# Handing a part's recurrences to the scheduler after 9 of 25 projection units instead of 13, at 2.5 steps per unit instead of 2

## The chip, the cores and the metric

The kernel runs on one core of a Trainium2 chip. The metric is the device time of one execution in microseconds; the times below are those of several executions, and the profile is of one more.

## The reference, cut to what matters

One layer over 2,048 tokens with 16 learned tokens ahead of them (T = 2,064) and a width of 1,024. The normalised input goes through one projection whose 3,080 columns are shared by three mixers; their outputs go through one output projection, and then follows a gated feed-forward net of width 2,816 with a depthwise convolution over time.

```python
p = rms_norm(h, norm_mix_pre) @ w_in
pa = p[..., :A_COLS]                    # RG-LRU group, 512 columns
pb = p[..., A_COLS:A_COLS + B_COLS]     # forgetting attention: q, k, v (512 each) and 8 gates
pc = p[..., A_COLS + B_COLS:]           # RWKV-7 group, 1024 columns
oa = rg_lru_group(xa, ya, ...)          # h_t = a_t * h_(t-1) + b_t, width 256
ob = forgetting_attention_group(...)    # 8 heads of 64, softmax(q k + c_i - c_j), causal
oc, v_own = rwkv7_group(pc, ...)        # S = S * w - (S kk) (kk a) + v k, 4 heads of 64x64
mixed = jnp.concatenate([oa, ob, oc], axis=-1) @ w_out
h = h + rms_norm(mixed, norm_mix_post)
f = causal_dwconv(rms_norm(h, norm_ffn_pre) @ ffn_up, ffn_conv)
h = h + rms_norm((gelu(gate) * val) @ ffn_down, norm_ffn_post)
```

The two recurrences (LRU and RWKV-7) run over time, so a block of tokens needs the state that the block before it left. RWKV-7 is computed in chunks of 64 tokens, whose inner triangular systems are solved by substitution.

## The kernel before, in words

Every large product is made in three matmuls of split operands (`mm3`, lines 170 to 174: high x high, high x low, low x high), recorded on TensorE under lines L172 to L174.

**The projection** (tile `psp`) runs in three parts of the tokens, each in two blocks of 400 and 384, of 384 and 384, and of 256 and 256 columns. A part is the generator `w_in_part` with 25 units: first the gates of attention (unit 1), then 8 column tiles of the RWKV group (kind "c", units 2 to 9), 4 of the LRU group (kind "a", units 10 to 13), 4 tiles of k, 4 of v and 4 of q; the last two units take one block each of the last two q tiles. The weight tile of a unit is split into a high and a low half in part 0 (`load_parts`, lines 161 to 167, ScalarE and VectorE) and stored; parts 1 and 2 load the halves again. Results leave PSUM over ScalarE or VectorE and go to DRAM (`scr_p`, `scr_v`, `scr_qh` and others).

**The recurrences** (PSUM tiles `rps` and `eps`) are the generator `recurrences`: two gate blocks of attention, then for each of three blocks of 256 tokens the first half of an RWKV block up to `R.SOLVED` (the raw rows of the projection are loaded, mixed with the token before, decays are made, the small triangular systems solved on GpSimd and VectorE with two round trips of DMA, `da` and `dx`), then the second half of the block before it (`R.ending`: the inverses of 64x64 by many 32x32 matmuls of line L1176, the state, the output), and then the LRU of the same block. Each `yield` ends a step. The last block (8) has 64 tokens.

`Beside` deals these steps out: `advance` is called once for each unit and takes `PACE` steps, as long as there are any. A part's recurrences are added to it when the unit READY + 1 of the same part has been made; in part 0, the first READY units are made ahead of the constants and of this loop. Steps that are left over go on with the units of the next part, and after part 2 `beside.finish()` and the loop over `R.ending` emit the rest.

**What emission decides.** The program is built with a scheduler: the order in which the code emits instructions is their priority, and the scheduler places them on the engines' queues by when it takes their operands to be ready. On the chip each engine then runs its queue in that order.

**Attention** (tiles `mx`, `sc`, `po`) is emitted after the recurrences. It runs in two halves: for all 8 heads the query blocks 0 and 1, and then for all heads the blocks 2 and 3, whose keys are twice as long. It takes the memory that the projection's pools leave. The output projection's weights (`woh`, `wol`, 16 loads of 512 KB, line L1480) and its PSUM take the space of the recurrences' pools (`rec.close()`); its tiles (`pswo`) are computed in the second half of attention, as attention makes their rows, and the last of them after it. After that come the feed-forward up (`psu`) and down (`psd`) products.

Of the kernel before, what the change touches and what calls it, by code (L numbers as in the profile page):

```python
# [438 lines left out]
class Attn:  # L439
# [43 lines left out]
    def next(self, s):  # L483
        self.turn[s] = (self.turn[s] + 1) % len(self.ring[s])
        return self.ring[s][self.turn[s]]
# [898 lines left out]
def lru_block(core, R, scr, k, b):  # L1384

    nc = core.nc
    t0 = max(0, Rwkv.start(b))
    n = min(T, Rwkv.start(b + 1)) - t0
    c0 = PAD + t0
    tt = nc.vector.tensor_tensor  # L1390
    stt = nc.vector.scalar_tensor_tensor

    def tl(s):
        return R.t([P, 256], s)[:, :n]

    def raw(row, a):
        t = R.t([P, 260], "lraw", bufs=2)[:, : c0 + n - a]
        nc.sync.dma_start(t, scr["p"][row : row + P, a : c0 + n])
        return t

    for p in range(2):
        pc = slice(p, p + 1)
        x = raw(P * p, c0 - 3)
        u, r, g, al = (tl("l" + s) for s in ("u", "r", "g", "a"))
        nc.scalar.activation(u, x[:, 3:], AF.Identity, scale=k["conv_w"][:, 6 + p : 7 + p], bias=k["conv_b"][:, pc])
        for i in range(3):
            stt(u, x[:, i : n + i], k["conv_w"][:, 2 * i + p : 2 * i + p + 1], u, op0=ALU.mult, op1=ALU.add)


        ps = R.pe()  # L1410
        pa, px = ps[:, :n], ps[:, 256 : 256 + n]
        nc.tensor.matmul(pa, k["ga_w"][:, p], u, start=True, stop=True)
        nc.tensor.matmul(px, k["gx_w"][:, p], u, start=True, stop=True)
        nc.scalar.activation(r, pa, AF.Abs, bias=k["ga_b"][:, pc])
        nc.vector.tensor_scalar(al, pa, k["ga_b"][:, pc], 0.0, op0=ALU.add, op1=ALU.min)
        nc.scalar.activation(g, px, AF.Tanh, scale=0.5, bias=k["rate"][:, 2, pc])
        nc.scalar.activation(r, r, AF.Tanh, scale=0.5)
        nc.scalar.activation(al, al, AF.Exp)
        stt(r, r, 1.0, al, op0=ALU.add, op1=ALU.mult)
        stt(g, g, 1.0, u, op0=ALU.add, op1=ALU.mult)  # L1420
        yield
        nc.scalar.activation(al, r, AF.Exp, scale=k["rate"][:, 0, pc])
        nc.scalar.activation(r, r, AF.Tanh, scale=k["rate"][:, 1, pc])

        tt(u, al, al, op=ALU.mult)
        stt(r, u, 1.0, r, op0=ALU.add, op1=ALU.mult)
        nc.vector.tensor_scalar(r, r, 1e-34, None, op0=ALU.max)
        nc.scalar.activation(r, r, AF.Sqrt)
        stt(g, g, 0.5, r, op0=ALU.mult, op1=ALU.mult)
        nc.vector.tensor_tensor_scan(u, al, g, k["h"][:, pc], op0=ALU.mult, op1=ALU.add)  # L1430
        nc.vector.tensor_copy(k["h"][:, pc], u[:, n - 1 : n])

        ya, y = raw(2 * P + P * p, c0), r
        nc.scalar.activation(y, ya, AF.Square)
        nc.vector.tensor_scalar(y, y, 0.044715, 1.0, op0=ALU.mult, op1=ALU.add)
        tt(y, y, ya, op=ALU.mult)
        nc.scalar.activation(y, y, AF.Tanh, scale=0.7978845608028654)
        stt(y, y, 1.0, ya, op0=ALU.add, op1=ALU.mult)
        stt(u, u, 0.5, y, op0=ALU.mult, op1=ALU.mult)
        nc.sync.dma_start(scr["mix"][P * p : P * p + P, t0 : t0 + n], u)  # L1440
        yield
# [466 lines left out]

READY = 13
PACE = 2.0

WIDE = (0, 5)

# [32 lines left out]
            pass  # L1948


def recurrences(core, R, lk, f_bias, scr, blocks, part):


    for blk in blocks:
        gate_block(core, R, f_bias, scr, blk[2])
        yield
    for b in ((0, 1, 2), (3, 4, 5), (6, 7, 8))[part]:
        gen = R.block(b)
        while next(gen) != R.SOLVED:
            yield  # L1960
        yield from R.ending
        R.ending = gen
        yield from lru_block(core, R, scr, lk, b)


# [10 lines left out]
def hybrid_block_kernel(ctx: ExitStack, tc: tile.TileContext, args, out):  # L1976
    a = {s: v[0] if s != "meta_tokens" else v for s, v in args.items()}
    nc = tc.nc
    core = Core(tc, ctx)
    scr = scratch(tc, ctx, core)  # L1980
# [4 lines left out]
    def run(gen):  # L1985
        for _ in gen:
            pass

    def pool(es, name, bufs, **kw):
        return es.enter_context(tc.tile_pool(name=name, bufs=bufs, **kw))  # L1990
# [11 lines left out]
    with ExitStack() as p1:  # L2002
        core.const = pool(p1, "const1", 1)
        dp = pool(p1, "dp", 2, space=DRAM)
        rec = ExitStack()
        ps_rw = pool(rec, "ps_rw", 2, space=PSUM, **right)
        ps_ae = pool(rec, "ps_ae", 1, space=PSUM, **right)
        gp = pool(rec, "gp", 1, **right)
        rp = pool(rec, "rp", 1, **right)
        with ExitStack() as p1a:  # L2010
            ps_mm = pool(p1a, "ps_mm", 5, space=PSUM)
            g_pre = spread(pool(p1a, "gpre", 1), a["norm_mix_pre"], "g_pre")
            pools = {"xn": pool(p1a, "xn", 1), "nt": pool(p1a, "nt", 4), "w": pool(p1a, "w", 2), "st": pool(p1a, "st", 2)}
            sums = up_sums(core, pool(p1a, "us", 1), a["ffn_up"], scr, EARLY)
            split_out = w_out_split(core, pools["nt"], a["w_out"], scr)
            following = w_in_norm(core, pools, ps_mm, x, meta, g_pre, 0)
            for part in range(3):
                blocks = following
                if part == 0:
                    zeros = pools["st"].tile([P, PAD], F32, tag="sth", name="zeros")  # L2020
                    nc.vector.memset(zeros[:], 0.0)
                    for r in range(0, A_ROWS + C_ROWS, P):
                        nc.gpsimd.dma_start(scr["p"][r : r + P, 0:PAD], zeros[:])
                units = w_in_part(core, pools, ps_mm, a["w_in"], blocks, scr, part)
                for _ in range(READY if part == 0 else 0):
                    next(units)
                if part == 0:
                    attn_consts(core)
                    rk = rwkv_consts(
                        core, gp, ps_ae,  # L2030
                        {
                            s[5:]: (v.rearrange("h d -> (h d)") if s == "rwkv_r_k" else v)
                            for s, v in a.items() if s.startswith("rwkv_")
                        },
                    )
                    lk = lru_consts(
                        core, gp, ps_ae,
                        {
                            "conv_w": a["lru_conv_w"], "conv_b": a["lru_conv_b"], "ga_w": a["lru_gate_a_w"],
                            "ga_b": a["lru_gate_a_b"], "gx_w": a["lru_gate_x_w"], "gx_b": a["lru_gate_x_b"],  # L2040
                            "lam": a["lru_lambda"],
                        },
                    )
                    columns(core, gp, ps_ae, [a["ffn_conv"].rearrange("i (r p) -> (i r) p", p=P)], "", cw)
                    R = Rwkv(core, rp, dp, ps_rw, ps_ae, scr, rk)
                    beside = Beside(PACE)
                for i, _ in enumerate(units, READY + 1 if part == 0 else 1):
                    if i == READY + 1:
                        beside.add(recurrences(core, R, lk, a["fox_f_bias"], scr, blocks, part))
                    beside.advance()  # L2050
                    if part and (i % 2 == 0 or part == 1 and i > 1):
                        with tc.issue_after(core.loaded.ins):
                            next(split_out if i % 2 else sums, None)
                run(sums) if part == 2 else None
                if part < 2:
                    following = w_in_norm(core, pools, ps_mm, x, meta, g_pre, part + 1)
        beside.finish()
        for _ in R.ending:
            pass
        rec.close()  # L2060
        p2 = ExitStack()
        ps_wo = [pool(p2, "ps_wo", 2, space=PSUM, **right)]
        with ExitStack() as p1b:
            more = pool(p1b, "ps_more", 1, space=PSUM, **right, **early)
            at = Attn(core, pool(p1b, "ap", 2, **early), pool(p1b, "ps_at", 1, space=PSUM), more, scr)

            pool(p1b, "pad", 1, **right).tile([P, 24832], F32, name="pad")
            at.run(pool(p1b, "mt", 1, **right, **early))
# [145 lines left out]
```

## Time and profile before

| what | value |
|---|---|
| median of the runs | 3072.16 us |
| lowest of the runs | 3068.99 us |
| span of the profiled execution (first to last instruction) | 3071.8 us |
| TensorE busy | 2921.6 us, 95% |
| VectorE busy | 2054.8 us, 67% |
| ScalarE busy | 1482.3 us, 48% |
| GpSimd busy | 1358.8 us, 44% |
| mean granted TensorE clock | 0.969 |
| moved by DMA | 532.58 MB, 173 GB/s in the mean |

The profile lists the span of its execution and no other time of it; the span lies 0.4 us from the median of the runs.

How the rows are read. In the page, each digit of a row of slices is the busy share of one fortieth of the span in tenths. A row of a stretch has its start and end, its length, then for each engine busy microseconds with the count of instructions, then the granted clock of TensorE, the share of the DMA engines and GB/s. A row of a tile has the least, the median and the greatest duration in ns, the first and the last start in us, and shapes. A row of waits reads: engine, tile and line of what waited, what ended the wait, microseconds in total, how often, the longest. PE is TensorE's matmul, PEld its weight load, DVE VectorE, ACT ScalarE, POOL GpSimd, SP SyncE, whose queue issues nearly all transfers. A matmul of plain float32 leaves two records.

### The profile page before, as it was taken

The numbers are of one execution on the slowest core, as the hardware profiler recorded it, in microseconds if no ns is written. First come the engines' busy times: TensorE is split into PE (matmuls) and PEld (weight loads), VectorE is DVE, ScalarE is ACT, GpSimd is POOL, SyncE is SP. The second block draws the span as 40 slices with busy tenths as digits, with TensorE's granted clock in tenths as the row PEclk, the third lists the DMA queues.
The fourth block names the chain that finished last, engine by engine and source line by source line (L and its number), as shares of the span: only waits on it lengthen the run. The fifth ranks groups of instructions, "written<-read, shape, count | busy, mean of one in ns | idle before, by whom it ended". The sixth has DMA issues, their size and how long they took to land. (4 is left out here: it accounts for less than half of the span.)

```text
span 3071.8 us, 52793 instructions
## 1 busy us (share of the span) xinstructions
PE 2921.6 (95%) x18694; PEld 2495.2 (81%) x18694; DVE 2054.8 (67%) x3934; ACT 1482.3 (48%) x2853; POOL 1358.8 (44%) x1589
## 2 busy tenths in 40 slices
PE   6999999999989999999989899999999999999998
PEld 6998898888876654665558899999999998787876
DVE  5268645656667785556635788888778786547766
ACT  4245332443336553555534656666566665324333
POOL 1001121122114555667842457445655444547765
PEclk9998999999988898999999999999999999999999
DMA  6776578466654346535245555566777765435444
GB/s 211 244 237 207 161 244 287 156 211 204 196 153 94 88 104 199 133 99 122 62 129 173 168 182 180 169 201 208 214 215 216 219 189 171 161 104 171 149 160 144
DMA packets 467818, 532.58 MB, mean 173 GB/s; under 512 B 85488, under 2 KB 355514, under 8 KB 466000
## 3 DMA queue, kind: packets, MB, share of 16 engines
q1 hardware_dynamic: 467168, 528.81, 56.5%
q8 instruction: 147, 2.41, 0.3%
q14 instruction: 119, 0.97, 0.1%
q0 software_dynamic: 384, 0.39, 0.0%
HBM read 369.11 MB, written 159.95 MB: 172 GB/s over the span
## 5 line engine op out<-in xcount | busy, mean ns | idle before, releaser
L172 PE MATMUL psu<-xo,uw 128*128 128x344 f32 x1848 | 589.9, 323 | 16.7 <-ACT xo L1594 6.9
L173 PE MATMUL psu<-xo,uw 128*128 128x344 f32 x1848 | 592.6, 321 | 0.0
L174 PE MATMUL psu<-xo,uw 128*128 128x344 f32 x1848 | 582.9, 320 | 0.0
L172 PE MATMUL psp<-xh,wh 128*128 128x384 f32 (+2 forms) x1152 | 383.6, 333 | 4.1 <-ACT wh L166 2.4
L174 PE MATMUL psp<-xh,wl 128*128 128x384 f32 (+2 forms) x1152 | 380.7, 331 | 3.5 <-DMA wl<-scr_wk 3.5
L173 PE MATMUL psp<-xl,wh 128*128 128x384 f32 (+2 forms) x1152 | 380.5, 330 | 0.0
L172 PEld LDWEIGHTS psu<-xo,uw 128*128 128x128 f32 x1848 | 346.9, 188 | 20.3 <-ACT xo L1594 7.1
L1595 DVE TENSOR_TENSOR uw<-uq,uw 128x512 fp32r<-128x512 f32 x341 | 316.2, 933 | 70.3 <-ACT uw L1594 63.7
L173 PEld LDWEIGHTS psu<-xo,uw 128*128 128x128 f32 x1848 | 347.9, 188 | 0.3 <-DVE xo L1595 0.3
L174 PEld LDWEIGHTS psu<-xo,uw 128*128 128x128 f32 x1848 | 346.5, 188 | 0.0
L1594 ACT ACTIVATE uw<-uq 128x512 fp32r<-128x512 f32 x462 | 287.9, 627 | 110.1 <-PE psu L174 48.7
L686 ACT ACTIVATE p<-sc,bias 128x512 f32<-128x512 f32 (+4 forms) x352 | 195.8, 590 | 178.5 <-PE sc L682 146.3
L1725 DVE SCALAR_TENSOR_TENSOR uy<-psu,ffn_cols,uy 128x342 f32<-128x342 f32 (+1 forms) x396 | 223.9, 567 | 60.7 <-ACT uy L1723 59.1
L559 DVE TENSOR_REDUCE mc<-mx 128x1 f32<-128x512 f32 (+6 forms) x352 | 190.3, 565 | 100.9 <-PE mx L554 75.8
L1731 POOL TENSOR_TENSOR uy<-uy,uy 128x342 f32<-128x342 f32 (+1 forms) x132 | 140.6, 1065 | 253.2 <-DVE uy L1725 77.4
L725 POOL TENSOR_TENSOR acc<-acc,p 128x512 f32<-128x512 f32 (+3 forms) x208 | 221.8, 1068 | 60.3 <-ACT p L686 23.9
L1595 POOL TENSOR_TENSOR uw<-uq,uw 128x512 fp32r<-128x512 f32 x121 | 177.9, 1470 | 125.0 <-ACT uw L1594 92.7
L174 PEld LDWEIGHTS psp<-xh,wl 128*128 128x128 f32 x1152 | 222.1, 193 | 13.0 <-issue 6.1
L172 PEld LDWEIGHTS psp<-xh,wh 128*128 128x128 f32 x1152 | 222.1, 193 | 10.7 <-issue 4.0
L173 PEld LDWEIGHTS psp<-xl,wh 128*128 128x128 f32 x1152 | 222.1, 193 | 7.6 <-issue 5.5
L1595 DVE TENSOR_TENSOR fo<-u,fo 128x896 fp32r<-128x896 f32 x88 | 112.6, 1279 | 121.3 <-ACT fo L1594 121.3
L1594 ACT ACTIVATE fo<-u 128x896 fp32r<-128x896 f32 x88 | 81.1, 922 | 206.3 <-POOL u L1841 106.8
(465 smaller groups left out, 6470.4 us busy)
## 6 DMA issues: line engine op xcount, KB each, us to landing
uq<-scr_us SPq DMA_DIRECT2D x220, 256.0 KB
uq<-in_ffn_up_dram SPq DMA_DIRECT2D x209, 256.0 KB
wl<-scr_wk SPq DMA_DIRECT2D x48, 512.0 KB
wh<-scr_wk SPq DMA_DIRECT2D x48, 512.0 KB
u<-scr_ff SPq DMA_DIRECT2D x88, 256.0 KB
scr_ff<-uy SPq DMA_DIRECT2D x110, 171.0 KB
raw<-in_w_in_dram SPq DMA_DIRECT2D x24, 512.0 KB
scr_wk<-wh SPq DMA_DIRECT2D x24, 512.0 KB
```

Source lines behind the costliest of these rows:

```text
L172: nc.tensor.matmul(out, ah, bh, start=first, stop=False, skip_group_check=more)
L173: nc.tensor.matmul(out, ah, bl, start=False, stop=False, skip_group_check=more)
L174: nc.tensor.matmul(out, al, bh, start=False, stop=last, skip_group_check=more)
L559: self.reduced = nc.vector.tensor_reduce(mc[:rows, i, ci : ci + 1], ps[:rows, : e - a], axis=AX.X, op=ALU.max)
L686: last = nc.scalar.activation(p[:rows, :w], ps[:rows, :w], AF.Exp, bias=bias[:rows, j : j + 1])
L725: eng.tensor_tensor(a, ps_[0][0][:rows, c0:n] if start and i == 1 else a, p[:rows, : n - c0], op=ALU.add)
L1594: core.nc.scalar.activation(hi, src, AF.Copy)
L1595: (eng or core.nc.vector).tensor_tensor(lo, src, hi, op=ALU.subtract)
L1725: stt(y[:, :n], src[:, i : n + i], cw[:, 44 * i + cc : 44 * i + cc + 1], y[:, :n], op0=ALU.mult, op1=ALU.add)
L1731: core.pooled = nc.gpsimd.tensor_tensor(v[:, :n], g[:, :n], v[:, :n], op=ALU.mult)
```

## The change

READY goes from 13 to 9, so a part's recurrences are added when unit 10 has been made and not unit 14; in part 0 the constants, too, are emitted after 9 units and not after 13. PACE goes from 2 to 2.5 steps for a unit. As the LRU needs the column tiles of kind "a", which are made in units 10 to 13, `recurrences` gets a list `made` with the units made in each part, and yields without work ahead of each LRU block while fewer than WHOLE = 13 are made. The arithmetic is the same.

```diff
-READY = 13
-PACE = 2.0
+READY = 9
+WHOLE = 13
+PACE = 2.5
...
-def recurrences(core, R, lk, f_bias, scr, blocks, part):
+def recurrences(core, R, lk, f_bias, scr, blocks, part, made):
...
         yield from R.ending
         R.ending = gen
+        while made[part] < WHOLE:
+            yield
         yield from lru_block(core, R, scr, lk, b)
...
             following = w_in_norm(core, pools, ps_mm, x, meta, g_pre, 0)
+            made = [0, 0, 0]
             for part in range(3):
...
                 for i, _ in enumerate(units, READY + 1 if part == 0 else 1):
+                    made[part] = i
                     if i == READY + 1:
-                        beside.add(recurrences(core, R, lk, a["fox_f_bias"], scr, blocks, part))
+                        beside.add(recurrences(core, R, lk, a["fox_f_bias"], scr, blocks, part, made))
                     beside.advance()
```

## The prediction

> **What bounds the kernel now.** I read the page first: the span, the busy shares and the slices of TensorE with its granted clock.
>
> ```profile
> span 3071.8 us, 52793 instructions
> PE 2921.6 (95%) x18694; PEld 2495.2 (81%) x18694; DVE 2054.8 (67%) x3934; ACT 1482.3 (48%) x2853; POOL 1358.8 (44%) x1589
> ...
> PE   6999999999989999999989899999999999999998
> ...
> PEclk9998999999988898999999999999999999999999
> ```
>
> TensorE is busy for 95% of the span and no other engine is above 67%, so the time is TensorE's work plus what it loses: 150 us idle, and some lowered clock, both mostly left of the middle. The clock's dip, slices 12 to 16 of about 77 us, is where the recurrences end. So I asked for busy time by stretch: start of the recurrences, the projection beside them, the first 53 us after the projection, the rest of the recurrences beside attention, the load of the output weights, and attention with output tiles.
>
> ```profile
> core 0: us, PE busy (x) PEld busy (x) DVE busy (x) ACT busy (x) POOL busy (x), PEclk, DMA share, GB/s
> 200.00:250.00 50.00, 50.00 (x300) 45.70 (x300) 33.75 (x85) 30.28 (x58) 8.26 (x16) 1.00 0.60 184
> 250.00:300.00 50.00, 42.73 (x291) 39.05 (x291) 42.91 (x117) 25.99 (x50) 4.40 (x6) 0.83 0.70 242
> 300.00:897.00 597.00, 577.52 (x5381) 521.77 (x5380) 351.85 (x884) 231.76 (x456) 118.67 (x194) 0.97 0.62 200
> 897.00:950.00 53.00, 40.52 (x347) 28.35 (x345) 45.20 (x118) 22.45 (x50) 21.84 (x29) 0.84 0.71 151
> 950.00:1148.00 198.00, 184.76 (x1651) 122.71 (x1644) 156.21 (x420) 116.64 (x252) 109.18 (x181) 0.91 0.36 91
> 1148.00:1202.00 54.00, 46.43 (x189) 22.63 (x188) 31.29 (x71) 16.35 (x32) 19.89 (x26) 0.75 0.87 256
> 1202.00:1400.00 198.00, 195.94 (x882) 122.70 (x882) 111.38 (x231) 98.81 (x178) 135.59 (x186) 1.00 0.44 110
> ```
>
> The columns are stretch, length, busy us with count, then granted clock. I call "loss" the idle time plus (1 - clock) times the length. It is 7.3 + 8.5 = 15.8 us in 250-300; 19.5 + 17.9 = 37.4 in 300-897, so 53 us for the projection from 200 on; 12.5 + 8.5 = 21 in 897-950; 13.2 + 17.8 = 31 in 950-1148 (15.7%); 7.6 + 13.5 = 21 in 1148-1202; and 2.1 in 1202-1400 (1%). Recurrence work beside attention thus loses most, attention alone almost nothing. The stage limits are in the rows of the single tiles:
>
> ```profile
> L174 PE MATMUL psp<-xh,wl x1152: 274/337/736, 42.5 to 896.0; 128*128 128x384 f32 x96, 128*128 128x256 f32 x64, 128*128 128x400 f32 x32
> ...
> L1034 PE MATMUL eps<-rwwa,wa_up x72: 272/376/502, 174.5 to 978.2; 64*128 64x256 f32 x64, 64*128 64x64 f32 x8
> ...
> L1321 PE MATMUL rps<-rwsg,g_up x36: 275/379/564, 373.2 to 1147.5; 128*128 128x256 f32 x32, 128*128 128x64 f32 x4
> ...
> L681 PE MATMUL sc<-q,k x352: 170/392/796, 908.8 to 1564.7; 128*128 128x512 f32 x112, 128*128 128x272 f32 x16, 128*16 128x16 f32 x16, 128*128 128x400 f32 x16
> ...
> L1480 SPq DMA_DIRECT2D woh<-scr_wo x8: 320/430/1478, 1164.1 to 1187.6; - x8
> ```
>
> The projection (psp) ends at 896, the recurrences (eps, rps) run from 174.5 to 1147.5, attention (sc) begins at 908.8, and the output weights, whose buffers need the recurrences' space, load from 1164.1.
>
> **The change part by part.** No instruction's work is added or removed; steps are moved in emission. Counted in the code: part 0 of the recurrences has 40 steps, parts 1 and 2 have 47 each, and 7 close the last block. Before, each part advances 12 units of 2 steps after its start and uses its other units for the backlog; 16 steps stay over after part 0, 23 after part 1, and 30 come after the last unit. After, 16 units of 2.5 steps give 40: about 1 and 7 stay over, and 14 come after the last unit. The wait for WHOLE costs one empty step, in part 0; later the previous block's seven closing steps carry the recurrence past unit 13 anyway.
>
> What counts is where the scheduler puts them. In the two built orders of TensorE I counted the matmuls of the recurrences and gates (2,304 in all) and of attention (1,762). Ahead of the last projection matmul stand 1,646 before and 1,745 after; by thirds of the projection 62, 697 and 757 become 246, 632 and 714. Behind it stand 658 recurrence matmuls among 610 of attention before, 559 among 364 after. So 30 steps less 14 come down to 99 matmuls. The front of block 7, few matmuls and a long chain on VectorE and GpSimd, is what mainly crosses. The first output-tile matmul stands behind 771 attention matmuls before, 720 after.
>
> The prices, rows of one tile each: rps for the projection and for the recurrences beside attention, then the same for eps.
>
> ```profile
> 150.00:897.00 747.00, 165.25 (x2935) 139.32 (x2936) 74.78 (x154) 40.27 (x80) 0.97 0.64 207
> 897.00:1148.00 251.00, 71.80 (x1232) 58.49 (x1228) 31.90 (x79) 14.57 (x31) 0.90 0.44 104
> ```
>
> ```profile
> 150.00:897.00 747.00, 62.51 (x223) 33.06 (x223) 22.86 (x56) 27.45 (x66) 0.97 0.64 207
> 897.00:1148.00 251.00, 10.86 (x40) 6.70 (x40) 4.02 (x11) 4.11 (x12) 0.90 0.44 104
> ```
>
> Beside the projection 227.8 us of TensorE for 1,646 is 0.138 us each; beside attention 82.7 us for 658 is 0.126. The same stretch 897-1148 for attention's mx, sc and po:
>
> ```profile
> 897.00:1148.00 251.00, 65.28 (x283) 30.39 (x215) 61.54 (x125) 18.35 (x29) 0.90 0.44 104
> ```
>
> ```profile
> 897.00:1148.00 251.00, 62.37 (x225) 37.17 (x226) 56.67 (x112) 0.90 0.44 104
> ```
>
> ```profile
> 897.00:1148.00 251.00, 48.65 (x206) 19.61 (x206) 8.65 (x14) 9.48 (x21) 0.90 0.44 104
> ```
>
> That is 176.3 us for 610, or 0.289 us each. The terms:
>
> (a) Work moved. 99 x 0.138 = +13.7 us in the projection, -99 x 0.126 = -12.4 us behind it. TensorE bounds both, so this is nearly a sum of zero.
>
> (b) Loss in the projection. 53 us beside 227.8 us of recurrence work is 0.23 per us: 13.7 x 0.23 = +3.2 us. Its bounds: 0, as the back half of block 0 (rich in matmuls) now stands at the change from part 0 to part 1 where the 250-300 row has VectorE at 42.9 of 50 and TensorE starved; and +31 us, worked out under the slower rival.
>
> (c) Loss beside attention. The remainder shrinks to 364 x 0.289 + 559 x 0.126 = 175.6 us of busy time; 251 us held 259 of it (matmuls overlap), so it lasts about 170 us. Without the first 53 us, whose loss is that of the change of stage and stays, 117 us x 15.7% = 18.4 us instead of 31: -12.7 us. The 246 attention matmuls that leave it, 71 us, then lose 1%: +0.7 us. Bounds: 0, if the loss goes with the recurrence matmuls and not with the time, and -31.
>
> (d) The load of the output weights. The rows of 1148-1202, waits and then DMA issues:
>
> ```profile
> POOL acc L725 <- DMA scr_den<-acc: 16.8, 2, 12.4
> ```
>
> ```profile
> woh<-scr_wo SPq DMA_DIRECT2D x8, 512.0 KB
> wol<-scr_wo SPq DMA_DIRECT2D x8, 512.0 KB
> ```
>
> 8.4 MB pass while attention's small transfers (one of them waits 12.4 us) and the longer keys of the second half of attention want the same DMA engines. On SyncE's queue 12 of the 16 loads before stand in nearly one run, behind the first head's keys of that second half; after, they begin about a head and a half earlier and stand dealt out between attention's loads. The same bytes still pass, so I take a third of the 21 us, -7; bounds 0 and -21.
>
> Sum: 13.7 - 12.4 + 3.2 - 12.7 + 0.7 - 7 = -14.5 us. The span of 3071.8 is 0.4 us from the median of the runs, 3072.16, and stands for it; no time of that execution is listed apart. 3071.8 - 14.5 = 3057.3, rounded 3057.
>
> [...] Two neighbouring stretches show the clock, and the timeline what stood ahead of them:
>
> ```profile
> 955.00:960.00 5.00, 5.00 (x91) 4.62 (x84) 4.50 (x12) 1.25 (x3) 2.10 (x7) 0.51 0.21 59
> 960.00:965.00 5.00, 5.00 (x17) 2.52 (x16) 1.92 (x6) 1.87 (x5) 0.96 (x3) 0.50 0.51 128
> ```
>
> ```profile
> 953.57 2.61 PE L1176 MATMUL rps<-rwxu 32*32 32x32 f32 x96 [1.64 <-DVE rwxu L1186]
> ```
>
> The clock is halved although TensorE shows no idle time; what ran ahead were 96 matmuls of 32x32 after only 1.64 us idle. [...] By the row the halving goes with the tiny matmuls, which each block brings wherever it stands, so I keep 15.7% of the shorter stretch.
>
> **The rivals.**
>
> *Nothing but the shift.* The loss follows the recurrences, (c) and (d) are nil: +13.7 - 12.4 + 3.2 = +4.5, 3076. For it: just 99 of 2,304 matmuls cross, and VectorE at 156.21 of 198 us (79%) in 950-1148 may pace the chain whatever attention does. Against it: the chain left behind the projection is one front half shorter.
>
> *Slower: evacuations and weight splits queue behind recurrence steps in part 0.* One wait shows the mechanism, at 261 us on TensorE, and the whole page shows how long ScalarE can stand at a recurrence instruction:
>
> ```profile
> 260.99 0.45 PE L172 MATMUL psp<-xh,wh 128*128 128x400 f32 x1 [2.42 <-ACT wh L166]
> ```
>
> ```profile
> ACT rwrav L1003 <- PE rps L1292: 36.6, 5, 17.9
> ```
>
> In part 0 ScalarE and VectorE also split each weight tile, and behind a waiting step on either queue stand that split and the PSUM evacuations; TensorE waits for both. The rate of undisturbed projection in part 0, psp alone:
>
> ```profile
> 50.00:150.00 100.00, 100.00 (x561) 100.00 (x560) 6.69 (x12) 5.99 (x12) 1.00 0.73 239
> ```
>
> 0.178 us each. The first recurrence matmul now comes after 524 instead of 713 projection matmuls. From there part 0 has 628 x 0.178 + 246 x 0.138 = 146 us; at the 32% loss of the 250-300 row it loses 46 us, 31 more than that row's 15.8. Then 3057 + 31 = 3088. It decides once part 0 loses over 14.5 us more than before. Against it: 200-250 holds 300 matmuls, recurrences among them, without loss. [...]
>
> *Larger gain.* The hole (d) goes wholly (-14 more) and the starved 250-300 too (-15.8), since block 0's matmuls stand there: 3057 - 30 = 3027.
>
> *Does nothing.* Excluded by the orders above, which differ from the 527th matmul on.
>
> **How the numbers follow.** Forecast (3040 to 3068) 0.45; only the shift, 3076, 0.22; slower, 3088, 0.20; larger gain, 3027, 0.10; 0.03 for the rest. The time is the forecast's, 3057. The range 3025 to 3092 reaches to both far cases with their bounds a little beyond; as cases of both signs hold chance, the forecast's own range stands above. A measurement here tells about 2%, 61 us, from no change. Faster by that would need (c), (d) and the 250-300 loss to vanish together: 0.03. Slower by that would need part 0 to lose over half of its 146 us: 0.05. The rest, 0.92, is within 2%.
>
> **What would show it.** The last psp matmul near 896 + 13.7 + 3 = 913; the last rps near 913 + 170 = 1083 instead of 1147; woh loading before attention's 720th matmul; the first pswo matmul earlier than now by about the gain; the clock up in the stretch behind the projection. The projection ending beyond 930, with ACT or DMA as releaser of psp, would mean the slower rival. A gap from last psp to last rps of 200 us or more would break (c); DMA near full with the clock at 0.75 after the last rps would break (d).

## The result and the profile after

The changed kernel takes 3089.97 us, the median of its runs (3081.16 to 3094.31), against 3071.85 us for the kernel before on the same chip: ratio 1.0052, 95% interval 1.0034 to 1.0069. That is within 2%, but longer by more than its interval, where 14.5 us less were forecast. One of the six runs of the kernel before took 4877.26 us and does not enter the ratio. The profiled execution took 3081.16 us and has a span of 3079.1 us; it is the shortest of the runs, and its span is only 7.3 us above that of before, so its trace can show less than half of the 18 us. Where a result is given as a ratio below, it is to the kernel before in runs on the same chip.

The page of the changed kernel, the lines that answer to the first ones of before:

```profile
span 3079.1 us, 52825 instructions
...
PE 2921.2 (95%) x18694; PEld 2502.8 (81%) x18694; DVE 2049.9 (67%) x3934; ACT 1483.0 (48%) x2853; POOL 1353.1 (44%) x1589
...
PEclk8999899999897999999999999999999999999999
```

TensorE's busy time is that of before within 0.4 us. Before, four of the slices 12 to 16 show a clock of 8; now only the eleventh and the thirteenth of that region are below 9, but the thirteenth (924 to 1001 us) shows 7. The rows of the single tiles say that the work was moved as forecast:

```profile
L174 PE MATMUL psp<-xh,wl x1152: 274/337/743, 42.4 to 912.1; 128*128 128x384 f32 x95, 128*128 128x256 f32 x64, 128*128 128x400 f32 x33
```

```profile
L1321 PE MATMUL rps<-rwsg,g_up x36: 275/379/483, 339.1 to 1088.3; 128*128 128x256 f32 x32, 128*128 128x64 f32 x4
```

```profile
L1480 SPq DMA_DIRECT2D woh<-scr_wo x8: 415/429/627, 1111.2 to 1144.0; - x8
```

```profile
L172 PE MATMUL pswo<-woh,mh x272: 387/389/796, 1192.7 to 1692.1; 128*128 128x512 f32 x128, 128*2 128x512 f32 x8
```

The projection ends at 912.1 (forecast 913), the recurrences at 1088.3 (forecast 1083), the output weights load from 1111 and not from 1164, and the first output tile starts at 1192.7, 10 us earlier than the 1202.7 of before. From the end of attention to the last instruction it is 1503.5 us before and 1506.6 after. So most of what this trace can show has to be sought between 37 and 1573 us.

I cut both kernels at the same points of their work: the three parts of the projection, the end of the projection, and the ends of attention's blocks 1, 10, 18 and 32 of 32 (the divisions on ScalarE, L738). Blocks in a range, as blocks 2 to 10, are attention's; block 5 and block 6 are blocks of the recurrence. First before, then after; columns as in the prediction (stretch, length, busy us with counts, granted clock).

```profile
37.90:299.80 261.90, 254.63 (x1481) 243.00 (x1479) 135.01 (x298) 109.77 (x195) 14.05 (x25) 0.97 0.71 231
299.80:630.10 330.30, 320.63 (x2719) 288.64 (x2717) 190.40 (x466) 120.73 (x228) 63.28 (x102) 0.98 0.65 212
630.10:896.00 265.90, 256.10 (x2650) 232.47 (x2649) 160.65 (x416) 110.52 (x226) 55.44 (x94) 0.96 0.58 187
896.00:940.70 44.70, 33.31 (x262) 23.71 (x261) 38.44 (x101) 14.39 (x35) 14.76 (x17) 0.81 0.79 166
940.70:1091.50 150.80, 140.37 (x1384) 94.63 (x1384) 118.87 (x329) 91.08 (x198) 84.23 (x142) 0.90 0.34 85
1091.50:1236.90 145.40, 133.13 (x695) 73.93 (x696) 96.58 (x218) 68.41 (x132) 78.57 (x110) 0.89 0.60 163
1236.90:1568.30 331.40, 321.50 (x1452) 193.72 (x1451) 183.50 (x366) 174.82 (x317) 238.81 (x304) 0.99 0.39 94
```

```profile
36.90:324.40 287.50, 279.03 (x1887) 260.84 (x1885) 167.52 (x389) 126.32 (x228) 22.45 (x41) 0.97 0.67 214
324.40:645.60 321.20, 309.12 (x2577) 284.07 (x2575) 179.80 (x444) 120.63 (x230) 61.84 (x103) 0.97 0.69 224
645.60:912.10 266.50, 257.80 (x2578) 233.05 (x2579) 160.77 (x415) 102.05 (x212) 48.43 (x78) 0.94 0.58 178
912.10:978.50 66.40, 55.97 (x562) 43.95 (x561) 50.71 (x143) 27.96 (x59) 20.29 (x33) 0.67 0.50 118
978.50:1103.30 124.80, 114.33 (x1025) 74.96 (x1025) 92.75 (x263) 74.45 (x162) 71.12 (x121) 0.97 0.39 97
1103.30:1243.90 140.60, 124.62 (x578) 69.72 (x578) 80.17 (x172) 64.06 (x124) 81.99 (x112) 0.93 0.64 170
1243.90:1572.50 328.60, 316.74 (x1433) 190.51 (x1433) 189.78 (x369) 175.45 (x319) 241.17 (x304) 0.99 0.38 94
```

With the prediction's loss (idle plus (1 - clock) times the length):

| stretch | loss before | loss after |
|---|---|---|
| part 0 of the projection | 15.1 | 17.1 |
| part 1 | 16.3 | 21.7 |
| part 2 | 20.4 | 24.7 |
| its end to block 1 | 19.9 | 32.3 |
| blocks 2 to 10 | 25.5 | 14.2 |
| blocks 11 to 18 | 28.3 | 25.8 |
| blocks 19 to 32 | 13.2 | 15.1 |
| sum | 138.7 | 151.0 |

The clock of a row has two digits, so a loss is open by up to 0.005 times the length, 1.7 us in the longest rows; differences of 2 us between such rows say nothing.

The projection got 17.1 us longer (sum of the first three lengths). Behind it only 11.9 us came back, where the forecast had 31.4. The rows to look at are the fourth and the fifth of each: the loss of blocks 2 to 10 fell by 11.3 us, and the stretch before them loses 12.4 us more, at a clock of 0.67. All of these 12.4 are clock (8.5 us before, 21.9 after); the idle time of the stretch fell from 11.4 to 10.4 us.

What that stretch consists of, from TensorE's timeline (in brackets the wait ahead of a group) and 5-us windows of the changed kernel:

```profile
923.99 3.59 PE L1176 MATMUL rps<-rwxu 32*32 32x32 f32 x96 [6.03 <-POOL rwitmp L1152]
...
937.25 1.97 PE L1216 MATMUL rps<-rww,rwsc 64*64 64x64 f32 x16
...
952.84 1.97 PE L1225 MATMUL rps<-rww,rwxf 64*64 64x128 f32 x8
```

```profile
917.00:922.00 5.00, 0.95 (x61) 0.84 (x54) 4.47 (x9) 2.53 (x6) 0.96 (x1) 0.99 0.67 166
922.00:927.00 5.00, 3.01 (x84) 3.04 (x85) 4.26 (x12) 0.00 (x0) 0.27 (x1) 0.50 0.76 186
...
942.00:947.00 5.00, 5.00 (x26) 3.61 (x25) 3.34 (x10) 4.20 (x10) 1.59 (x3) 0.50 1.09 214
...
957.00:962.00 5.00, 5.00 (x31) 3.77 (x27) 3.40 (x12) 1.14 (x3) 2.21 (x5) 0.50 0.01 3
962.00:967.00 5.00, 5.00 (x60) 4.22 (x61) 2.83 (x9) 0.36 (x2) 0.05 (x1) 0.58 0.13 13
```

The second half of block 6 (the 32x32 inversions of L1176 and the 64x64 matmuls of L1216 and L1225) now stands right behind the projection: in the emitted order 251 recurrence matmuls come between the projection's last matmul and attention's fiftieth, 95 before. Near its start stands a wait of 6.03 us for the triangular solve, and from then on the granted clock is 0.50 for some 40 us, although from 937 on TensorE has work recorded in all of each window. (Whether the wait started it is taken up with the load of the output weights below.)

### The profile page after: what moved, and what is told of

Read it like the earlier page. It is cut to its first block, busy times and chain, and to the rows that moved or that the text cites. A ratio compares the mean times of both kernels' runs of the same rounds, so it can differ in the third digit from the quotient of the medians.

```text
span 3079.1 us, 52825 instructions
## 1 busy us (share of the span) xinstructions
PE 2921.2 (95%) x18694; PEld 2502.8 (81%) x18694; DVE 2049.9 (67%) x3934; ACT 1483.0 (48%) x2853; POOL 1353.1 (44%) x1589
## 4 chain that ended last, share of the span: by engine, by line
PE 35%; DMA 5%; DVE 4%; POOL 3%; issue 2%; ACT 1%; SPq 0%; POOLq 0%; DVEq 0%; ACTq 0%
PE psu L172 8%; PE psu L173 8%; PE psu L174 8%; PE psd L173 2%; PE psd L172 2%; PE psd L174 2%; DMA u<-scr_ff 2%; DMA xt<-scr_h 1%; PE pswo L174 1%; PE pswo L172 1%; PE pswo L173 1%; DVE fo L1595 1%; DVE uw L1595 1%; POOL u L1840 1%; POOL u L1838 1%
## 5 line engine op out<-in xcount | busy, mean ns | idle before, releaser
L172 PEld LDWEIGHTS psu<-xo,uw 128*128 128x128 f32 x1848 | 347.6, 189 | 19.9 <-ACT xo L1594 7.1
```

The costliest lines, as they stand in the source:

```text
L172: nc.tensor.matmul(out, ah, bh, start=first, stop=False, skip_group_check=more)
```

## The experiments

All measured kernels in one table. The clock is the median of the mean granted clock over the timed runs of that kernel; the kernel before, run beside each group of experiments, has 0.971 every time.

| kernel | READY, PACE | ratio | interval | clock |
|---|---|---|---|---|
| the change | 9, 2.5 | 1.0052 | 1.0034 to 1.0069 | 0.966 |
| the change again | 9, 2.5 | 1.0061 | 1.0039 to 1.0084 | 0.966 |
| early start alone | 9, 2 | 1.0081 | 1.0058 to 1.0103 | 0.963 |
| pace alone | 13, 2.5 | 0.9990 | 0.9974 to 1.0006 | 0.970 |
| slower pace alone | 13, 1.5 | 1.0091 | 1.0068 to 1.0114 | 0.9625 |
| load held back | 9, 2.5 | 1.0040 | 1.0021 to 1.0059 | 0.969 |
| early in part 0 | 9/13/13, 2.5 | 1.0043 | 1.0026 to 1.0060 | 0.9665 |
| early in parts 1, 2 | 13/9/9, 2.5 | 1.0053 | 1.0034 to 1.0071 | 0.966 |
| early in parts 0, 1 | 9/9/13, 2.5 | 0.9987 | 0.9970 to 1.0003 | 0.970 |
| early in part 2 | 13/13/9, 2.5 | 0.9979 | 0.9962 to 0.9996 | 0.972 |
| sixteen dense | 9, 2.5 | 1.0032 | 1.0014 to 1.0049 | 0.968 |
| sixteen narrow | 9, 2.5 | 1.0036 | 1.0022 to 1.0050 | 0.969 |
| dense in two blocks | 9, 2.5 | 1.0012 | 1.0001 to 1.0024 | 0.971 |

To 0.001, the last column orders the ratios. From 0.971 to 0.966 the same work would take 3072 x (0.971 / 0.966 - 1) = 16 us longer, if all of it went with the clock; that is an estimate, and the two ratios of the change give 16 and 19 us. So what the change loses over many runs is, by its size, mostly granted clock.

**The change again, and before again.** First whether the difference and its place repeat. The edit is none.

> The changed kernel unchanged, for a second profile and for the spread of its times. In the first profile its projection ends 16 us later than before, the end of attention is 4 us later and the last instruction 7 us later, while the median of its runs is 18 us above that of before. Theory 1 (what is lost is lost by the end of attention, the first profile was a lucky run): the second profile shows attention ending 12 us or more later than before. Theory 2 (the feed-forward products lose it, where the order of instructions also differs): attention ends again 4 us later and the rest is 8 us or more longer than before. Time 3090 +- 5 by both.

> The kernel before, for a second profile: how far the milestones (end of the projection, end of attention, end) lie apart in two profiles of one kernel. In the two profiles of the change the end of the projection differs by 3 us and the end of attention by 10 us. Expected the same here, and 3062 to 3084 us.

The change again: 3092.58 us (3081.65 to 3098.85), span of the profile 3084.4; before again: 3073.76, span 3072.0. The projection ended at 915.4 and 892.4; from there to attention's last block it was 667.0 and 674.0 us; the stretch to block 1 had the same length, 66.5 us, and the same clock, 0.67, and 45.3 us at 0.81 before. Attention ended at 1582.4, 14 us later than in the first profile of before, and from there to the last instruction it was 1502.0 us (1505.6 in before again), so the feed-forward stage is out as a cause.

**Early start or pace.**

The first edit is against the change, the second against the kernel before.

```diff
 READY = 9
 WHOLE = 13
-PACE = 2.5
+PACE = 2.0
```

```diff
 READY = 13
-PACE = 2.0
+PACE = 2.5
```

> READY 9 with the wait for 13, but 2.0 steps per unit as before: the early start alone. 580 recurrence matmuls stand behind the projection (658 before, 559 after), the last of them behind 424 attention matmuls (610, 364). If the early start makes the loss (recurrence steps beside the weight splits of part 0): 3085 to 3093. If the pace makes it: 3070 to 3075. If it is just the shift that is given back later: 3072 to 3077.

> READY 13 as before with 2.5 steps per unit: the pace alone. 616 recurrence matmuls behind the projection, the last behind 551 attention matmuls. If the early start makes the loss: 3070 to 3075. If the pace makes it: 3082 to 3092.

The early start alone takes 3097.01 us (3085.51 to 3104.59), the pace alone 3066.92 (3065.55 to 3083.45); they lie 4 us above and 3 us below the ranges that were expected if the early start costs. The pace is not what costs: with the start at 13 units it is even with before. In its profile the projection ends at 905.5 and attention 655.6 us later, 16.7 less than before.

**The load of the output weights.** The loads are queued behind the keys of the tenth of attention's sixteen passes over a head (`keyed` collects those loads of keys), so that they start when they did before.

```diff
-            w = w_out_load(core, wp, scr)
+            with tc.issue_after(at.keyed[9].ins):
+                w = w_out_load(core, wp, scr)
```

> The changed kernel with the 16 loads of the output weights queued behind the tenth head's keys, where they stand before the change; the order of TensorE up to the first output tile stays that of the change, the first output tile comes after 783 attention matmuls instead of 720 (771 before). In the first profile of the change attention loses 18 us more between its 10th and 14th query block, where these loads now run, and makes it up until the 17th. If the new place of the loads costs the time: 3076 to 3082. If that stretch is made up anyway: 3088 to 3092.

3082.64 us (3075.02 to 3103.16). The load is back at 1163, and blocks 11 to 18 have this row:

```profile
L1481 SPq DMA_DIRECT2D woh<-scr_wo x8: 348/430/642, 1163.2 to 1187.7; - x8
```

```profile
1103.30:1232.50 129.20, 113.51 (x542) 60.14 (x542) 77.12 (x169) 62.79 (x122) 77.94 (x107) 0.96 0.65 175
```

15.7 idle and 5.2 of clock are 20.9 us of loss, against 25.8 in the change and 28.3 before. The early load thus gained nothing; the intervals of the two ratios overlap, so that it cost something isn't shown either.

Up to the first output tile TensorE's order is here that of the change, so this is a third trace of the stretch behind the projection:

```profile
911.60:978.20 66.60, 57.39 (x562) 45.36 (x560) 50.66 (x143) 28.07 (x58) 20.23 (x33) 0.62 0.50 118
```

```profile
912.00:917.00 5.00, 3.13 (x22) 2.60 (x24) 4.78 (x7) 3.97 (x8) 5.00 (x3) 0.78 0.31 69
917.00:922.00 5.00, 1.75 (x64) 1.61 (x62) 4.32 (x11) 2.87 (x6) 0.49 (x1) 0.50 0.68 156
```

The half-clock stretch is there too, at 0.62 over the whole of it. It begins between 912 and 917 us, ahead of the wait for the solve (4.76 us here, up to 923.51) and with no idle time above 1.09 us ahead of it. So here the wait did not start it. And with all of that stretch in it, this execution took 3078.2 us.

**Which part.** READY is made one number per part.

```diff
-READY = 9
+READY = (9, 13, 13)     # or (13, 9, 9), (9, 9, 13), (13, 13, 9)
...
-                    if i == READY + 1:
+                    if i == READY[part] + 1:
```

> The changed kernel with the early start in part 0 alone (after 9 units there, after 13 in parts 1 and 2; 2.5 steps per unit). Part 0 gets 246 recurrence matmuls as in the change, but 616 stand behind the projection as with the pace alone (559 in the change, 658 before). Theory P (the early start in part 0 makes the loss, wherever the matmuls end up): 3085 to 3095. Theory C (what costs is that recurrence matmuls are taken from beside attention, 99 of them for +18 us): 3066 to 3074, as with the pace alone.

> The other half: part 0 starts after 13 units as before, parts 1 and 2 after 9; 2.5 steps per unit. 62 recurrence matmuls in part 0, 543 behind the projection, the last behind 383 attention matmuls. Theory P: 3064 to 3074. Theory C: 3088 to 3096, with 115 matmuls taken from beside attention.

Beside them, the start at 13 units with fewer steps, so that more is left behind the projection:

```diff
-READY = 9
+READY = 13
-PACE = 2.5
+PACE = 1.5
```

> READY 13 with 1.5 steps per unit: less of the recurrences beside the projection than before, 859 matmuls behind it. If work moved from one place to the other is a sum of about zero, the projection ends at 868 (201 x 0.138 us earlier than 896) and attention 25 us more than before behind that, and the time is 3068 to 3078. Theory C: 3045 to 3065. If the loss beside attention grows with the time that recurrences run there, as the prediction took it (15.7% of it): 3085 to 3095.

Early in part 0 alone: 3086.95 us (3080.62 to 3099.93). Early in parts 1 and 2: 3090.92 (3086.73 to 3095.89). Each costs as much as both together, so the loss is no sum over parts. The slower pace, which leaves 859 recurrence matmuls behind the projection instead of 658, takes 3104.81 (3091.33 to 3110.83): its projection ends at about 858, and then attention needs 741.8 us instead of 672.3. That is more than any of the three expectations had. Too much behind the projection costs as well.

> The change, but in part 2 the recurrences wait for 13 units again (READY is 9, 9, 13; 2.5 steps per unit everywhere). In the emitted order 70 recurrence matmuls then stand between the end of the projection and the fiftieth attention matmul (251 in the change, 95 before), and 621 in all behind the projection (559 and 658). Theory T (what the change loses, it loses where attention starts: part 2's early start hands a block of small recurrence matmuls to the stretch right behind the projection, which then runs at half clock): the loss from the projection's end to attention's first block falls back from 32 us to 20-27 us, the clock there is above 0.75, and the median is 3075-3083 us. Theory P (the loss is made in parts 0 and 1, where the recurrences fight the weight splits): 3086 us or more, as with part 0 alone (3087), and a loss in the projection of 60 us or more. Neither is excluded in part: then both show, at 3083-3088.

> The early start in part 2 alone (READY is 13, 13, 9; 2.5 steps per unit). Only 40 recurrence matmuls stand between the projection's end and the fiftieth attention matmul, 583 behind the projection in all. Theory T: the half clock behind the projection comes from the block of recurrence matmuls that lands there, not from the early start as such; here little lands there, so the loss from the projection's end to attention's first block is at most 25 us and the median 3062-3075 us, not slower than the kernel with 2.5 steps and no early start (3067). Theory P: parts 0 and 1 are as in that kernel, so 3065-3070, with the projection's loss near 57 us. Against both: if an early start in part 2 costs by itself, whatever lands where, it is 3080-3090 and the loss at attention's start is 30 us or more.

Early in parts 0 and 1: 3065.81 us (3058.43 to 3076.25). Early in part 2 alone: 3061.77 (3058.01 to 3072.67), the shortest of all, and 0.2% below before. So the early start in itself has no price: of the six kernels that differ from before in the start, with or without the pace, and in nothing else, four are 0.4 to 0.8% longer than before, and two are not longer at all. The first is shorter than any of its expectations had it. Part 2 of the projection and the two stretches behind it in the first, and then of the second the stretch behind the projection and blocks 11 to 18:

```profile
643.30:892.10 248.80, 238.21 (x2459) 216.09 (x2459) 145.40 (x366) 94.02 (x191) 50.36 (x77) 0.98 0.60 189
892.10:933.10 41.00, 27.77 (x197) 20.32 (x195) 34.30 (x88) 15.75 (x39) 12.36 (x15) 0.75 0.82 181
933.10:1088.10 155.00, 141.34 (x1379) 98.00 (x1379) 120.85 (x323) 89.35 (x193) 78.62 (x136) 0.89 0.31 80
```

```profile
909.00:951.40 42.40, 27.67 (x196) 20.36 (x196) 33.66 (x93) 20.19 (x44) 12.42 (x17) 0.76 0.80 180
1097.00:1221.60 124.60, 115.17 (x617) 63.83 (x617) 77.10 (x192) 63.84 (x126) 71.79 (x102) 0.97 0.65 181
```

With few recurrence matmuls behind the projection (70 and 40 up to attention's fiftieth) the loss there is 23.5 and 24.9 us, not 32.3. But in the first the loss of blocks 2 to 10 is 30.7, so that both stretches together have 54.2 against 46.5 in the change: what this kernel saves, it saves in part 2 of the projection, which takes 248.8 us and not 266.5. Of these 17.7 us, 62 x 0.138 = 8.6 are recurrence matmuls that it leaves behind (621 and not 559), and 9.1 are loss (15.6 and not 24.7, from the first of these rows). In the second it is blocks 11 to 18, which lose 13.2 us and not 25.8. And early in part 0 alone, which has only 73 matmuls in that place, takes 3086.95 us nonetheless: its trace loses 25.2 us in the stretch behind the projection and 35.1 in blocks 2 to 10, 22.0 of it clock. The count of matmuls behind the projection, by itself, does not forecast the time.

**Does the half clock make the time?** The next three add work to the change: sixteen bf16 matmuls that stream 512 columns each, written ahead of the first L1216 group of block 6 to the same PSUM tile, which is then overwritten. They are 128 columns of weights wide, or 32, or stand in blocks 5 and 6.

```diff
         for i0 in range(0, ni, 8):
             m = min(8, ni - i0)
             ps = self.ps().rearrange("p (i t) -> p i t", t=64)
+            if b == 6 and i0 == 0:           # or b in (5, 6)
+                wide = core.futureb[:].rearrange("p (o t) -> p o t", o=1).to_broadcast([P, 4, P])
+                for _ in range(16):          # or identb[:, 0:32] into ps[0:32]
+                    nc.tensor.matmul(ps.rearrange("p i t -> p (i t)"), core.identb[:], wide, start=True, stop=True)
```

> The change, with sixteen additional 128x512 bf16 matmuls in front of the second half of block 6's first output matmuls, written to the same PSUM tile, which is then overwritten: added work, nothing left out. Question: does a short dense run of large matmuls bring the clock back from 0.50 in the stretch right behind the projection? If the clock there is low because the matmuls are small and thin, it is at 0.9 or more within 10 us behind the sixteen, the stretch from the projection's end to attention's first block loses 10 us less of clock and pays about 4-7 us for the sixteen: 3083-3090 us against the change's 3090-3093. If the low clock is a span of fixed length once it has been granted, the stretch stays at 0.50 for some 40 us and the run is 4-8 us slower than the change: 3094-3100 us.

3079.50 us (3071.57 to 3091.27). The profiled execution is one of its longest, 3090.07. Its timeline and its windows:

```profile
942.71 6.21 PE L1218 MATMUL rps<-futureb,identb 128*128 128x512 bf16 x16
...
949.83 1.09 PE L1220 MATMUL rps<-rww,rwsc 64*64 64x64 f32 x16
...
956.99 1.08 PE L1229 MATMUL rps<-rww,rwxf 64*64 64x128 f32 x8
```

```profile
942.00:947.00 5.00, 5.00 (x26) 2.18 (x24) 3.72 (x12) 4.13 (x8) 2.66 (x6) 0.50 0.82 177
947.00:952.00 5.00, 5.00 (x47) 3.54 (x46) 2.95 (x10) 3.70 (x7) 1.51 (x2) 0.90 1.04 226
...
957.00:962.00 5.00, 5.00 (x32) 3.78 (x30) 3.29 (x14) 2.84 (x7) 2.08 (x5) 0.62 0.60 117
```

The groups that took 1.97 us in the change take 1.09 and 1.08: the clock is back as the sixteen end. But the order of the later instructions is not that of the change (the scheduler places them by their durations), so the order could be the cause of the shorter time. Nor does this trace show the time that is saved. The stretch behind the projection and blocks 2 to 10:

```profile
917.50:982.00 64.50, 54.74 (x573) 40.53 (x572) 49.92 (x143) 27.16 (x57) 19.82 (x32) 0.71 0.52 122
982.00:1125.70 143.70, 126.89 (x1031) 84.82 (x1030) 97.65 (x263) 75.41 (x163) 70.98 (x121) 0.87 0.34 84
```

The first loses 18.7 us of clock, against 21.9 in the change and not 10 us less, since the clock falls again; the second takes 143.7 us, against 124.8. The median is below both ranges that were expected, but its ratio, 1.0032, overlaps in its interval with those of the change and of the load held back (1.0040), which has the half-clock stretch whole. The narrow sixteen have the order of the dense ones, instruction for instruction.

> The kernel with the sixteen 128x512 matmuls, but with 32 columns of weights instead of 128 (so a quarter of the array works; the same 512 columns stream through). Every engine's order is that of the kernel with the full sixteen. If what brings the clock back is a dense run of large matmuls, the clock stays at 0.50 behind these sixteen, until about 40 us after it fell, and the median is 7-12 us above the 3079.5 us of the full sixteen. If it is only that TensorE streams long columns without a gap, it is back at 0.9 or more behind the sixteen, as it was at 948 us with the full ones, and the medians agree within 4 us. If the shorter time came from the order that the sixteen gave, and not from the clock, the medians agree too, but the clock stays low.

3081.29 us (3078.19 to 3087.51), like the dense ones.

```profile
942.00:947.00 5.00, 5.00 (x16) 1.88 (x16) 4.00 (x13) 4.09 (x8) 2.82 (x6) 0.63 0.83 188
947.00:952.00 5.00, 5.00 (x57) 4.43 (x54) 3.60 (x15) 3.37 (x7) 1.26 (x3) 1.00 1.07 223
952.00:957.00 5.00, 4.71 (x25) 3.21 (x23) 2.19 (x8) 2.59 (x9) 0.00 (x0) 0.56 0.45 122
```

The clock comes back here too. So a quarter of the weight columns was enough; sixteen short matmuls in the same place were not tried. As clock and order agree in both kernels, this pair did not part the two.

> The change, with sixteen additional 128x512 matmuls at the same place of block 5 as of block 6: block 5 is the one whose recurrence crosses the end of the projection's fourth fifth at half clock (from 823 us, 8 to 10 us of clock lost in all four profiles of this order). If the half clock is the loss and a dense run ends it, part 2 of the projection gets no longer in spite of the sixteen (266 us or less) and the median is 3074-3080 us. If the projection's own matmuls bring the clock back there anyway (it is at 0.65 to 0.69 between 830 and 850 us), the sixteen only cost their 4 to 6 us: 3080-3086 us.

3071.49 us (3068.49 to 3086.21), clock 0.971 in the median of its runs: with 32 matmuls more than the change, 12 to 15 us of its loss are gone (1.0012 against 1.0052 and 1.0061; the intervals are clear of each other), more than either range expected. TensorE's order differs from the change's here too, from block 5's second half on. The first output tile stands behind 720 attention matmuls, as in the change. Part 2 of the projection and the stretch behind it:

```profile
647.50:910.40 262.90, 253.84 (x2594) 228.31 (x2595) 162.18 (x417) 103.73 (x214) 47.87 (x77) 0.97 0.57 181
910.40:969.00 58.60, 50.73 (x570) 37.41 (x569) 42.76 (x134) 25.39 (x55) 21.16 (x33) 0.77 0.59 133
969.00:1101.60 132.60, 123.13 (x1033) 80.62 (x1032) 95.14 (x271) 74.93 (x163) 72.85 (x122) 0.91 0.36 92
```

Part 2 is 3.6 us shorter than in the change and the stretch behind it 7.8; in this execution blocks 2 to 10 take 7.8 longer, so up to block 10 only part 2's gain is left. Nor is the profile a proof for block 5. In the change, the clock is low there for most of 30 us, and in this kernel it is up before its sixteen come at 841.75 (the change first):

```profile
825.00:830.00 5.00, 4.71 (x79) 4.25 (x77) 2.42 (x9) 1.36 (x3) 2.01 (x6) 0.50 0.94 268
830.00:835.00 5.00, 5.00 (x91) 4.44 (x93) 2.38 (x7) 1.67 (x4) 1.73 (x5) 0.69 1.01 371
...
845.00:850.00 5.00, 5.00 (x42) 4.44 (x40) 2.42 (x8) 3.13 (x7) 0.00 (x0) 0.68 0.52 168
```

```profile
825.00:830.00 5.00, 4.45 (x80) 4.02 (x78) 2.25 (x10) 1.64 (x4) 1.87 (x6) 0.68 0.92 258
830.00:835.00 5.00, 4.38 (x107) 3.76 (x108) 3.28 (x10) 1.67 (x4) 2.14 (x5) 1.00 0.99 383
```

What is shown: the change's runs have a lower granted clock, to about the amount of their loss; a half-clock stretch of some 40 us stands where the change put block 6's second half, in all three traces of this order; sixteen long matmuls end it (0.50 to 1.00); and the kernel that has them in two blocks has the clock and, to 0.1%, the time of before. Not shown: that the end of this stretch by itself makes the shorter time, since each of the three kernels with added matmuls also has another order, and orders alone move the ratio between 0.998 and 1.009; how the 16 to 19 us divide over the places, since executions of one kernel lie up to 28 us apart (load held back) and the profile of the change catches its shortest; and why early in part 0 alone loses as much, in other places.

## Why the prediction was wrong, point by point

**(a) and (b), the projection: the sum held, by luck.** +16.9 us were forecast, 17.1 measured, the end at 912.1 against 913. But by the table the loss went from 51.8 us to 63.5, so +11.7 and not the +3.2 of (b), and what is left for the moved work is 5.4 us and not the 13.7 of (a). Read in windows of 5 us, where the two digits of the clock weigh less, the losses are 52.3 and 62.1 and the two shares 9.8 and 7.3. Two errors of 6 to 9 us cancelled. Most of the added loss is clock (25.1 to 34.2 by the table). (b) priced the loss by the amount of recurrence work; yet part 2 has fewer recurrence matmuls than before (714 and not 757) and no less loss, and part of that loss stands in one place, the second half of block 5 at a clock of 0.50 to 0.69 (the rows from 825 to 850 us above).

**(a) behind the projection: about held.** All terms together shortened this part by 11.9 us. The loss in it went from 86.9 us to 87.4, so by the table that is work alone: 12.4 us, as forecast (the two digits of the clock leave some 3 us of it open). The rest of the forecast's 31.4 us, the loss that was to go, did not go in the sum.

**(c) failed, at "whose loss is that of the change of stage and stays".** The price for the rest was about right: blocks 2 to 10 lost 11.3 us less, 12.7 forecast (6.6 us less between the two second executions). But the loss of the change of stage was 19.9 and became 32.3 us (21.1 and 32.6 in the second executions), so the two stretches together lose 46.5 us where they lost 45.4. I had subtracted 53 us as a fixed cost and not asked which steps would fill them: with 14 steps left and not 30, block 6's second half is first in line, and the clock is 0.50 from 922 to 962 us, while its small matmuls run. The line that the prediction named for this, the gap from last psp to last rps under 200 us, was met at 176.2; it is no measure of the time, as the work that left it was paid for elsewhere. "The clock up in the stretch behind the projection" was the sign that would have told, and it went from 0.81 to 0.67.

**(d) failed in size.** The load moved as forecast, but blocks 11 to 18 lost 25.8 us and 29.1 in the second execution (15.0 idle, 14.1 of clock), after 28.3 before; and holding the load back did not lengthen the time. What is lost there is not set by the load's place on SyncE's queue alone. With (c) and (d) some 17 of the 22 us are named that lie between the forecast and this trace; both profiles of the change, 3081.16 and 3086.43 us, are shorter than its medians, and where the rest of the 18 us goes stays open.

**The row of the halved clock.** It was a guide, as what runs at 0.50 in the change is again a block of tiny matmuls, but it is not the whole. In the change the half clock follows an idle wait of 6.03 us. In the load held back it stands ahead of that wait, behind idle times of 1.09 us at most, and in dense in two blocks the clock is 0.69 from 915 to 920 us and 0.50 from 920 to 925, behind idle times of 1.55 us at most from 910 on: in these two no wait of 6 us stood ahead of it. But small recurrence matmuls did not always stand ahead of it either: the change's clock is also 0.50 from 1155 to 1160 us, where attention runs alone.

```profile
1155.00:1160.00 5.00, 4.06 (x12) 2.45 (x11) 3.80 (x8) 1.50 (x3) 3.21 (x5) 0.50 0.82 193
```

Recorded work alone did not bring the clock back: in the change TensorE has 5.00 of 5.00 us busy in window after window, at 0.50 from 937 to 962. The dense sixteen of 6.21 us did: in windows of 2 us the clock is 0.50 up to 948 us and 1.00 from there to 958.

**The rivals.** "Nothing but the shift" had the mechanism behind the projection nearly right (no loss comes back), as a sum over its stretches, with 3076 for a time; it missed the clock in the projection. "Slower: evacuations and weight splits queue behind recurrence steps in part 0" is refuted as a mechanism: part 0's loss went from 15.1 to 17.1 us (22.2 in the second execution, 10.5 idle and 11.7 of clock), short of the 14.5 more from which it would decide, and the projection did not end beyond 930. In early in part 0 alone part 0 loses 21.8 us, 19.8 with the pace alone, so that kernel does not lose its time there either. Its 3088 is close to the result for another reason. "Larger gain" did not occur.

**A count of the prediction.** Its thirds of the projection add up to 1,516 and 1,592 recurrence matmuls, not to its 1,646 and 1,745. The other 130 and 153 stand between two parts, as the traces show recurrence matmuls there too; no term of the sum uses the thirds.

## What to carry to other kernels

When work is moved to fill an idle stretch, ask which instructions will stand first in each stretch afterwards, and do not carry a stretch's loss over as a constant: here that of the change of stage went from 19.9 to 32.3 us with other instructions in it. A block of many small matmuls ran at a clock of 0.50 for 40 us here, the last 25 of them with 5.00 of 5.00 us recorded busy, and sixteen long matmuls in it brought 1.00, so it is worth trying where long matmuls stand between them. A change made in one part (early in part 2 alone: 0.2% below before) may gain where the change in all parts loses. Compare the mean granted clock over many runs before explaining 0.5% from one trace.

## What the hardware showed that I had not expected

In the change the granted clock stayed at 0.50 for some 40 us (922 to 962), the last 25 of them with work recorded all the time, and 6.21 us of long matmuls brought it to 1.00 (from 948 us on), as did 5.47 us that used a quarter of the weight columns (1.00 from 947 to 952). After those it fell again (0.62 and 0.56 in the windows from 957 and 952), once more among 64x64 matmuls. Over the runs of a kernel the mean granted clock goes from 0.961 to 0.968 (the change again), and its longest run, 3098.85 us, has the lowest.
